# Adding the down projections' results to the residual by accumulating DMAs instead of VectorE

## The chip, the core and the metric

The kernel runs on one core of a Trainium2 chip. A core has a matrix engine (TensorE, PE in the profile, with its weight loads as PEld), a vector engine (VectorE, DVE), a scalar engine (ScalarE, ACT), GpSimd (POOL), and a queue processor (SyncE, SP). Each engine works through its own instruction list in order and waits on semaphores of the others. Data moves between the chip's memory and the on-chip SBUF, and inside SBUF, by 16 DMA engines; a transfer can be issued from SP, ACT or POOL. TensorE writes its sums into eight PSUM banks of 128 partitions x 512 fp32.

The metric is the device time of one execution, in microseconds (us), lower is better. Three runs of the kernel before took 1739.26, 1739.81 and 1739.86 us; the median is 1739.81 us. A separate execution was profiled.

## The reference

One layer on an input of 256 tokens x 2048 columns, fp32: a half-step SwiGLU feed-forward block, a mixer, a second half-step feed-forward block, and a final norm. The change touches only the line that adds a feed-forward block's result to the residual `x`, which runs twice:

```python
def swiglu_ffn(x, w_gate, w_up, w_down):
    return (jax.nn.silu(x @ w_gate) * (x @ w_up)) @ w_down

x = x + 0.5 * swiglu_ffn(rms_norm(x, ffn1_norm), ffn1_w_gate, ffn1_w_up, ffn1_w_down)
...                                    # mixer: x = x + y @ w_out
x = x + 0.5 * swiglu_ffn(rms_norm(x, ffn2_norm), ffn2_w_gate, ffn2_w_up, ffn2_w_down)
return rms_norm(x, final_norm)
```

`w_gate` and `w_up` are 2048 x 5632, `w_down` is 5632 x 2048.

## The kernel before

The residual stays on chip for the whole run, in one SBUF tile `xres` of 128 partitions x 2 token halves `t` x 2048 columns, cut into four column chunks `c` of 512. So one piece `xres[:, t, c]` is 128 x 512 fp32, 256 KB.

All weights are read once, as 1 MB blocks `raw` of 512 x 512, issued from SP. Each block is split for precision into a high part `hi` (a cast on ScalarE, two instructions of 128 x 1024) and a low part `lo` (a subtraction on VectorE, one instruction of 128 x 2048); TensorE multiplies with both (`multiply`). So ScalarE and VectorE must deliver a split block for every few microseconds of TensorE's work, and `raw` and split tiles come from pools of two to five buffers.

A feed-forward block `ffn(tag, ...)` runs through the 5632 hidden columns in six parts: a first chunk of 512, then five stages `s` of 1024. Each stage computes gate and up products with a seven-multiplication scheme (`seven`). After the stages `s` = 0, 2, 4 `down(last)` multiplies the hidden columns gathered so far with their rows of `w_down`, and adds half of the result to the residual. There are thus six down stages, three for each block. One down stage does, in the order of the code:

1. `product` for column chunk `c` = 0: two banks `ps_d`, one for each token half; then `update(0, t, ps)`.
2. `seven_of` prepares the sums of hidden blocks for the seven-multiplication scheme (`hspare` and eight `hs` tiles).
3. `seven` for the chunks 1 and 2 at once, in four banks `a`, `c`, `e`, `d`. On the way ScalarE copies four intermediate sums out of the banks (`snap`: `s1`, `s5`, `u2`, `u3`). When two banks of a chunk are complete (`done`, here `add`), `update` adds the bank and its snapshots to the residual: chunk 1 takes bank `c` with `u2` and bank `e` with `u3` and `s5`, chunk 2 takes bank `d` with `s1` and bank `a` alone.
4. `product` for `c` = 3 and `update(3, t, ps)`.

So in each down stage VectorE runs 12 instructions `xres = 0.5 * part + xres`: eight with a bank and four with a snapshot as the part.

`hspare`, `hs`, the snapshots and several tiles of the gate and up products are allocated with `keep(...)`, from one pool of 13 tiles of 128 x 512 fp32. A new tile waits until one of the 13 has had its last reader.

Instructions are not issued strictly in the order of the code: a planner orders each engine's list by program priority and by planned durations, and it places the semaphore waits. Only where `Engine.pinned` is true does an instruction keep its place in program order: in the opening, and from the last `product` of the second block on.

In the last down stage of each block `update` also calls `after(c, t)`. In the first block that is `to_mixer`, which defers the mixer norm's work on this chunk: squares of `xres` on ScalarE (`junk_nm`), and TensorE transposes of `xres` (`pt_nm`), which the mixer's first products read. In the second block it is `last`: squares on ScalarE (`junk_f`), for chunks 0 to 2 a VectorE scaling of `xres` by the final gain `fin`, after chunk 2 a partial sum `pre` and its root on ScalarE, and for chunk 3 the rest of the final norm and the stores of the output.

Of the kernel before, what the change touches and what calls it, by code (L numbers as in the profile page):

```python
# [12 lines left out]
AF = mybir.ActivationFunctionType  # L13
ALU = mybir.AluOpType
# [9 lines left out]
CW = 512  # L24
NC_D = D // CW
# [23 lines left out]
def hybrid_block(ctx: ExitStack, tc: tile.TileContext, a: dict, out: bass.AP):  # L49
    nc = tc.nc  # L50
    Engine.pinned = False
    dve, act, pe = (Engine(tc, e) for e in (nc.vector, nc.scalar, nc.tensor))
# [29 lines left out]
    def bank(name):  # L82
        return psum.tile([P, 512], F32, tag="ps", name=name)
# [74 lines left out]
    def load(src, name, pieces=((0, UK),), loaded=None, kept=False):  # L158
        if kept is None and extra and not turn_of["hold"]:
            turn_of["raw"] += 1  # L160
            kept = turn_of["raw"] % 5 > 2
        if kept:
            raw = extra[1].tile([P, UK, CW], F32, tag="kept", name=f"raw_{name}", bufs=2)
        else:
            raw = raws.tile([P, UK, CW], F32, tag="raw", name=f"raw_{name}")
        for i, e in pieces:
            nc.sync.dma_start(raw[:, i:e, :], src[i * P : e * P].rearrange("(j p) c -> p j c", p=P))
            if loaded:
                loaded(i)
        return raw  # L170

    def parts_of(raw, name, pieces=((0, 2), (2, UK)), split=None):
        pool, bufs = splits, 2
        if extra:
            turn_of["split"] += 1
            if turn_of["split"] % 3 == 0:
                pool, bufs = extra[0], 1
        hi = pool.tile([P, UK, CW], F32R, tag="hi", name=f"hi_{name}", bufs=bufs)
        lo = pool.tile([P, UK, CW], F32R, tag="lo", name=f"lo_{name}", bufs=bufs)
        for i, e in pieces:  # L180
            if split:
                split(i)
            act.copy(hi[:, i:e, :], raw[:, i:e, :])
            if split:
                dve.tensor_tensor(lo[:, i:e, :], raw[:, i:e, :], f32(hi[:, i:e, :]), op=ALU.subtract)
        if not split:
            dve.tensor_tensor(lo, raw, f32(hi), op=ALU.subtract)
        return [(hi[:, j, :], lo[:, j, :]) for j in range(UK)]
# [8 lines left out]
    def multiply(targets, blk, apart=False, middle=None):  # L197


        more = dict(skip_group_check=True) if apart else {}  # L200
        for ps, st, begin, _ in targets:
            for j in range(UK):
                pe.matmul(ps, st[j][0], blk[j][0], start=begin and j == 0, stop=False, **more)
                pe.matmul(ps, st[j][1], blk[j][0], start=False, stop=False, **more)
        if middle:
            middle()
        for ps, st, _, end in targets:
            for j in range(UK):
                pe.matmul(ps, st[j][0], blk[j][1], start=False, stop=end and j == UK - 1, **more)
# [141 lines left out]
    def quad(tile):  # L351
        return tile.rearrange("p (j c) -> p j c", j=UK)

    def seven(w, rows, cols, sf, xs, name, keep, done, between=None, ready=None):


        a, c, e, d = (bank(f"ps_{name}_{n}") for n in "aced")

        def get(u, n, kept=False):
            src = w[u * UK * P : (u + 1) * UK * P, cols[n] : cols[n] + CW]  # L360
            return load(src, f"{name}_{u}{n}", kept=kept)

        (r0, r1), two = rows, len(xs) > 1
        w11, first = ready or (get(r0, 0, True), None)
        w12 = get(r0, 1, True)
        b2, w22 = get(xs[0][0], 1), get(r1, 1)
        b3 = get(xs[1][0], 1) if two else None
        a2, w21 = get(xs[0][0], 0), get(r1, 0)
        a3 = get(xs[1][0], 0) if two else None

        def snap(ps, n):
            s = keep(f"{n}_{name}")
            act.copy(s, ps)
            return s

        def product_of(i, raw, ps, begin=False, end=True, blk=None):
            multiply([(ps, sf[i], begin, end)], blk or parts_of(raw, f"{name}_p{i}"), True)

        def usual(i, raw, n, *targets):

            blk = parts_of(raw, f"{name}_x{i}{n}")
            multiply([(ps, stationary(xs[i][1], t), b, z) for ps, t, b, z in targets], blk, True)

        product_of(0, w11, a, True, blk=first)
        s1 = snap(a, "s1")
        dve.tensor_tensor(w11, w12, w11, op=ALU.subtract)
        product_of(4, w11, c, True)
        s5 = snap(c, "s5")
        if between:
            between(0)  # L390
        usual(0, b2, 1, (e, 1, True, not two), (c, 0, False, False))
        if between:
            between(1)
        dve.tensor_tensor(w11, w22, w11, op=ALU.subtract)
        product_of(5, w11, a)
        u2 = snap(a, "u2")
        if between:
            between(2)
        if two:
            usual(1, b3, 1, (e, 1, False, True), (c, 0, False, False))  # L400
        dve.tensor_tensor(w12, w22, w12, op=ALU.subtract)
        product_of(6, w12, a)
        u3 = snap(a, "u3")
        done(1, 1, e, [u3, s5])
        product_of(2, w22, c)
        done(0, 1, c, [u2])
        usual(0, a2, 0, (d, 0, True, False), (a, 1, False, False))
        dve.tensor_tensor(w11, w21, w11, op=ALU.subtract)
        product_of(3, w11, a, end=not two)
        if two:  # L410
            usual(1, a3, 0, (a, 1, False, True), (d, 0, False, False))
        done(1, 0, a, [])
        product_of(1, w21, d)
        done(0, 0, d, [s1])

    def ffn(tag, norm, after, opening=False):
        with (
# [5 lines left out]
            wg, wu, wd = (a[f"ffn{tag}_w_{s}"][0] for s in ("gate", "up", "down"))  # L423

            def keep(name, dt=F32):
                return fp.tile([P, CW], dt, tag="keep", name=name, bufs=13)

            hidden = {}
# [24 lines left out]
            units, vs, sf, ready = [], {}, {}, []  # L453
# [36 lines left out]
            ps = {(m, t): bank(f"ps_{m}{tag}_0_{t}") for m in "gu" for t in range(NT)}  # L490
# [161 lines left out]
            xs = list(enumerate(units))[2:]  # L652
            turn_of["hold"] = False

            def down(last):
                us = sorted(set(hidden) | {w[0] for w in waiting})
                m, n = us[-2:]

                def update(c, t, *parts):
                    xr = xres[:, t, c * CW : (c + 1) * CW]  # L660
                    for p in parts:
                        dve.scalar_tensor_tensor(xr, p, 0.5, xr, op0=ALU.mult, op1=ALU.add)
                    if last:
                        after(c, t)

                for c in (0, 3):
                    end = last and tag == 2 and c == NC_D - 1
                    ps = product(
                        wd, c, us[:-2] + [n, m], hidden.get, f"d{tag}_{m}_{c}", end,
                        (lambda i: settle()) if c == 0 else None,  # L670
                    )
                    Engine.pinned = end
                    for t in range(NT):
                        update(c, t, ps[t])
                    if c == 0:
                        sh = {}
                        seven_of(
                            sh, hidden[m], hidden[n],
                            {(t, i): turned[u, t] for t in range(NT) for i, u in ((0, m), (1, n))},
                            quad(keep(f"hspare{tag}_{m}")),  # L680
                            [[quad(keep(f"hs{tag}_{m}_{i}_{z}", F32R)) for z in range(2)] for i in range(4)],
                        )()
                        got = {}

                        def add(t, b, ps, tiles):
                            got[t, b] = [ps] + tiles
                            if (0, b) in got and (1, b) in got:
                                for i in range(NT):
                                    update(2 - b, i, *got[i, b])

                        if tag == 1 and m == 5:
                            prepare()
                        seven(wd, (m, n), (2 * CW, CW), sh, [(u, hidden[u]) for u in us[:-2]], f"d{tag}_{m}", keep, add)
                hidden.clear()
                turned.clear()

# [78 lines left out]
    with tc.tile_pool(name="mixer", bufs=1) as mp, tc.tile_pool(name="mixw", bufs=2) as mw:  # L775
# [180 lines left out]
        for i, (use, part, half) in enumerate(order):  # L956
            ps = columns(w_in, part * (D // 2) + half * CW, nm.xT, f"in_{part}_{half}")
# [15 lines left out]
        for c in range(NC_D):  # L973
            cs = slice(c * CW, (c + 1) * CW)
            for g in range(2):
                if c == 0 and g == 1:
                    flush()
                ps = product(w_out, c, (2 * g, 2 * g + 1), yT.__getitem__, f"o{c}_{g}")
# [9 lines left out]
                for t in range(NT):  # L988
                    xr = xres[:, t, cs]
# [81 lines left out]
```

## Time and profile before

| | |
|---|---|
| median of 3 runs | 1739.81 us (1739.26 to 1739.86) |
| the profiled execution | 1741.48 us |
| its span, from the first to the last instruction | 1739.7 us |
| mean granted TensorE clock | 0.999 |
| last down stage of the first block | about 625 to 712 us |
| last down stage of the second block | about 1645 to 1731 us |

The profile is a record of one execution. Busy time counts an engine's instructions, without the issuing of DMAs from SP and ACT. A row of instructions reads: line, engine, operation, output<-inputs, shape, count, then busy us in all, mean ns of one, and the idle time of the engine just before them with what ended it. Nearly all instructions carry line 42, the line of the helper that records them, so they are told apart by their tiles; `ps_d` are the banks of the products for chunks 0 and 3, `ps_d_a`, `ps_d_c`, `ps_d_e`, `ps_d_d` those of the seven-multiplication scheme in a down stage.

### The profile page before, as it was taken

How to read it: one execution, taken by the hardware profiler on the slowest of the kernel's cores; microseconds unless marked ns; L12 is line 12 of the kernel's file. 1: busy time of each engine (PE TensorE's matmuls, PEld its weight loads, DVE VectorE, ACT ScalarE, POOL GpSimd, SP SyncE). 2: the span in 40 equal slices, each digit the busy share in tenths (PEclk: the TensorE clock that was granted, in tenths of full speed). 3: DMA queues.
4: the chain of work that ended last, by engine and by line, in shares of the span. 5: the costliest groups of instructions: out<-in, count | busy, mean ns of one | idle time of the engine just before them, and what ended most of it. 6: DMA issues, size and time to landing. Idle time of an engine off the chain costs nothing. (4 is left out here: it accounts for less than half of the span.)

```text
span 1739.7 us, 20328 instructions
## 1 busy us (share of the span) xinstructions
PE 1721.9 (99%) x8035; PEld 1436.1 (83%) x8035; DVE 1485.2 (85%) x1233; ACT 1042.1 (60%) x1345; POOL 6.9 (0%) x32
## 2 busy tenths in 40 slices
PE   8999999999999999999999999999999999999997
PEld 6888888888888888888888888888788888888886
DVE  7998999889789898687986668989799888899895
ACT  6765566656466656565655555656556664656654
POOL 1000000000000000000000000000000000000000
PEclk9999999999999999999999999999999999999999
DMA  8564665575466656555556663575475546555742
GB/s 299 191 213 145 218 214 197 182 254 205 159 209 203 199 188 216 172 170 194 177 189 209 224 203 129 199 243 185 160 252 201 206 144 231 193 194 194 255 174 104
DMA packets 173920, 343.24 MB, mean 197 GB/s; under 512 B 5636, under 2 KB 8064, under 8 KB 173696
## 3 DMA queue, kind: packets, MB, share of 16 engines
q1 hardware_dynamic: 173360, 340.82, 57.2%
q8 instruction: 63, 1.03, 0.2%
q10 hardware_dynamic: 144, 1.05, 0.1%
q14 instruction: 33, 0.27, 0.0%
q0 software_dynamic: 320, 0.07, 0.0%
HBM read 339.82 MB, written 2.10 MB: 197 GB/s over the span
## 5 line engine op out<-in xcount | busy, mean ns | idle before, releaser
L42 ACT CAST hi_g_p<-raw_g 128x1024 fp32r<-128x1024 f32 x132 | 134.3, 1049 | 97.8 <-DVE raw_g L42 27.6
L42 ACT CAST hi_u_p<-raw_u 128x1024 fp32r<-128x1024 f32 x140 | 140.8, 1047 | 73.1 <-DVE raw_u L42 26.8
L42 DVE TENSOR_TENSOR lo_g_p<-raw_g,hi_g_p 128x2048 fp32r<-128x2048 f32 x66 | 150.2, 2285 | 30.2 <-ACT hi_g_p L42 29.9
L42 DVE TENSOR_TENSOR lo_u_p<-raw_u,hi_u_p 128x2048 fp32r<-128x2048 f32 x70 | 159.0, 2286 | 19.3 <-ACT hi_u_p L42 18.9
L42 PE MATMUL ps_d<-hi_d,h 128*128 128x512 f32 x704 | 168.0, 390 | 0.0
L42 PEld LDWEIGHTS ps_d<-hi_d,h 128*128 128x128 f32 x704 | 131.5, 188 | 27.0
L42 PE MATMUL ps_in<-xT_nm,hi_in 128*128 128x512 f32 x640 | 153.3, 391 | 0.0
L42 PEld LDWEIGHTS ps_in<-xT_nm,hi_in 128*128 128x128 f32 x640 | 117.4, 188 | 23.3 <-ACT tha L42 0.3
L42 ACT CAST hi_d<-raw_d 128x1024 fp32r<-128x1024 f32 x88 | 88.2, 1047 | 68.2 <-PE ps_u_d L42 22.4
L42 DVE TENSOR_TENSOR lo_d<-raw_d,hi_d 128x2048 fp32r<-128x2048 f32 x44 | 100.6, 2290 | 31.0 <-ACT hi_d L42 31.0
L42 DVE TENSOR_TENSOR lo_in<-raw_in,hi_in 128x2048 fp32r<-128x2048 f32 x40 | 91.3, 2286 | 38.8 <-ACT hi_in L42 38.2
L42 ACT CAST hi_in<-raw_in 128x1024 fp32r<-128x1024 f32 x80 | 80.0, 1045 | 67.1 <-PE ps_in L42 45.8
L42 ACT CAST hi_d_p<-raw_d 128x1024 fp32r<-128x1024 f32 x84 | 84.3, 1047 | 50.2 <-DVE raw_d L42 39.4
L42 ACT CAST hi_g_x<-raw_g 128x1024 fp32r<-128x1024 f32 x80 | 81.3, 1048 | 47.5 <-PE ps_g_c L42 25.3
L42 DVE TENSOR_TENSOR lo_d_p<-raw_d,hi_d_p 128x2048 fp32r<-128x2048 f32 x42 | 95.4, 2286 | 11.8 <-ACT hi_d_p L42 11.7
L42 ACT CAST hi_u_x<-raw_u 128x1024 fp32r<-128x1024 f32 x80 | 80.5, 1047 | 33.9 <-PE ps_u_c L42 21.8
L42 DVE TENSOR_TENSOR raw_u<-raw_u,raw_u 128x2048 f32<-128x2048 f32 x40 | 91.6, 2290 | 9.0 <-DMA raw_u<-in_ffn_w_up_dram 8.3
L42 DVE TENSOR_TENSOR lo_g_x<-raw_g,hi_g_x 128x2048 fp32r<-128x2048 f32 x40 | 91.3, 2284 | 5.5 <-ACT hi_g_x L42 5.3
L42 DVE TENSOR_TENSOR raw_g<-raw_g,raw_g 128x2048 f32<-128x2048 f32 x37 | 84.5, 2286 | 9.3 <-DMA raw_g<-in_ffn_w_gate_dram 8.9
L42 DVE TENSOR_TENSOR lo_u_x<-raw_u,hi_u_x 128x2048 fp32r<-128x2048 f32 x40 | 91.4, 2284 | 0.8 <-ACT hi_u_x L42 0.5
L42 PE MATMUL ps_d<-lo_d,h 128*128 128x512 f32 x352 | 87.3, 389 | 0.0
L42 PEld LDWEIGHTS ps_in<-xT_nm,lo_in 128*128 128x128 f32 x640 | 82.1, 191 | 3.1
(391 smaller groups left out, 3592.2 us busy)
## 6 DMA issues: line engine op xcount, KB each, us to landing
raw_d<-in_ffn_w_down_dram SPq DMA_DIRECT2D x88, 1024.0 KB, 5.1
raw_u<-in_ffn_w_up_dram SPq DMA_DIRECT2D x87, 1024.0 KB, 5.2
raw_g<-in_ffn_w_gate_dram SPq DMA_DIRECT2D x86, 1024.0 KB, 5.2
raw_in<-in_w_in_dram SPq DMA_DIRECT2D x40, 1024.0 KB, 5.0
raw_o<-in_w_out_dram SPq DMA_DIRECT2D x16, 1024.0 KB, 5.1
xres<-in_x_dram SPq DMA_DIRECT2D x4, 512.0 KB, 7.6
raw_u<-in_ffn_w_up_dram SPq DMA_DIRECT2D x2, 512.0 KB, 9.3
raw_g_first<-in_ffn_w_gate_dram SPq DMA_DIRECT2D x1, 1024.0 KB, 11.9
```

The lines of the kernel that those rows point to most:

```text
L42: ins = getattr(self.engine, name)(*args, **kwargs)
```

## The change

For all pieces but `c` = 3 of the last down stage of either block (`last` is true for stage `s` = 4 of both), `update` no longer uses VectorE. ScalarE writes half of the bank into a new tile `half` of the 13-tile pool, and GpSimd issues one DMA for each part (first the snapshots, then `half`), which adds the part to the piece of `xres`. The snapshots of a down stage are halved as ScalarE takes them out of the banks (`scale=0.5`), so they can be added as they are. `after(c, t)` is called as before, right behind, and reads what the DMAs left.

```diff
-    def seven(w, rows, cols, sf, xs, name, keep, done, between=None, ready=None):
+    def seven(w, rows, cols, sf, xs, name, keep, done, between=None, ready=None, scale=None):
...
         def snap(ps, n):
             s = keep(f"{n}_{name}")
-            act.copy(s, ps)
+            if scale:
+                act.activation(s, ps, AF.Copy, scale=scale)
+            else:
+                act.copy(s, ps)
             return s
...
-                def update(c, t, *parts):
+                def update(c, t, ps, *tiles):
                     xr = xres[:, t, c * CW : (c + 1) * CW]
-                    for p in parts:
-                        dve.scalar_tensor_tensor(xr, p, 0.5, xr, op0=ALU.mult, op1=ALU.add)
+                    if last and c == NC_D - 1:
+                        dve.scalar_tensor_tensor(xr, ps, 0.5, xr, op0=ALU.mult, op1=ALU.add)
+                    else:
+                        half = keep(f"half{tag}_{m}_{c}_{t}")
+                        act.activation(half, ps, AF.Copy, scale=0.5)
+                        for p in (*tiles, half):
+                            nc.gpsimd.dma_start(xr, p, accum_op=ALU.add)
                     if last:
                         after(c, t)
...
-                        seven(wd, (m, n), (2 * CW, CW), sh, [(u, hidden[u]) for u in us[:-2]], f"d{tag}_{m}", keep, add)
+                        seven(wd, (m, n), (2 * CW, CW), sh, [(u, hidden[u]) for u in us[:-2]], f"d{tag}_{m}", keep, add, scale=0.5)
```

## The prediction, made before the changed kernel ran

> **What bounds the kernel now.** First the page's busy times, then the engines' busy time by stretches (the first 10 us, the body, the end), then TensorE's and its weight loads' waits inside the body.
>
> ```profile
> PE 1721.9 (99%) x8035; PEld 1436.1 (83%) x8035; DVE 1485.2 (85%) x1233; ACT 1042.1 (60%) x1345; POOL 6.9 (0%) x32
> ...
> 10.00:1725.00 1715.00, 1711.80 (x7997) 1428.07 (x7997) 1476.99 (x1212) 1033.11 (x1327) 1.05 (x16) 1.00 0.58 197
> 1725.00:1739.70 14.70, 5.85 (x26) 4.50 (x24) 5.15 (x14) 4.28 (x10) 0.00 (x0) 0.83 0.39 143
> ...
> PE ps_d_a L42 <- DVE lo_d_p L42: 1.1, 2, 0.9
> PE ps_g_c L42 <- DVE lo_g_p L42: 0.7, 1, 0.7
> PE ps_g_a L42 <- ACT hi_g_p L42: 0.3, 1, 0.3
> ...
> PEld ps_d_a L42 <- DVE lo_d_p L42: 2.6, 4, 1.3
> PEld ps_d_a L42 <- ACT hi_d_p L42: 0.7, 4, 0.2
> ```
>
> TensorE is busy for 1711.80 of the body's 1715.00 us, at a granted clock of 1.00. So 3.2 us are idle there, and that is the most that any relief of VectorE can return in the body (0.18% of the span). The row that the change can help directly is `ps_d_a <- lo_d_p`: TensorE waits for VectorE's splits in the down stages, 1.1 us by its own row, 2.6 us by the weight loads' row. The weight loads run ahead of the matmuls, so only the smaller is surely lost time. The end stretch holds the last chunk's norm and stores; chunk 3 of the last stage stays as it is, so it changes only if something earlier arrives late.
>
> VectorE at 85% looks like a second bound, but TensorE's three rows sum to 2.1 us, and one of them is ScalarE's: nearly all of VectorE's lateness is hidden.
>
> **What is removed.** The residual's additions on VectorE:
>
> ```profile
> L42 DVE SCALAR_TENSOR_TENSOR xres<-ps_d,xres x24: 677/682/692, 159.8 to 1730.9; 128x512 f32<-128x512 f32 x24
> ...
> L42 DVE SCALAR_TENSOR_TENSOR xres<-u_d,xres x12: 680/684/687, 179.6 to 1694.8; 128x512 f32<-128x512 f32 x12
> L42 DVE SCALAR_TENSOR_TENSOR xres<-s_d,xres x12: 677/682/692, 180.8 to 1713.7; 128x512 f32<-128x512 f32 x12
> ...
> L42 DVE SCALAR_TENSOR_TENSOR xres<-ps_d_e,xres x6: 680/684/692, 168.8 to 1688.0; 128x512 f32<-128x512 f32 x6
> ...
> L42 DVE SCALAR_TENSOR_TENSOR xres<-ps_d_a,xres x6: 678/686/692, 190.8 to 1705.8; 128x512 f32<-128x512 f32 x6
> ```
>
> With the banks `c` and `d` (six each, like `e` and `a`) that is 24 + 12 + 12 + 4 x 6 = 72; four stay (chunk 3 of the two last stages). 68 x 0.683 = 46 us leave VectorE. Two of them stand just ahead of the stretch where TensorE waits for `lo_d_p`, so I take the gain between 0 and 2.6 us, and as value 1.3, near the 1.1 us of TensorE's own row: half of the waits' chain is the splits themselves, which stay.
>
> **What ScalarE gets.** 48 - 4 = 44 new copies with a scale from a bank, and a scale on 24 snapshots. The nearest rows are the snapshot itself and an activation from a bank:
>
> ```profile
> L42 ACT COPY u_d<-ps_d_a x12: 574/579/589, 173.6 to 1690.1; 128x512 f32<-128x512 f32 x12
> ...
> L42 ACT ACTIVATE z<-ps_g_a 128x512 f32<-128x512 f32 x10 | 6.0, 600 | 33.7 <-PE ps_g_a L42 33.7
> ...
> 1393.00:1480.00 87.00, 87.00 (x389) 72.12 (x388) 73.34 (x51) 47.22 (x54) 0.00 (x0) 1.00 0.53 183
> ```
>
> 44 x 0.58 to 0.60 = 26 us, some 4.7 us for each down stage of eight copies. The last row is the third down stage of the three in the second block's middle: of 87 us ScalarE is busy for 47, so there is room for it, and the 20 ns by which the two rows differ come to 0.5 us over 24 snapshots, all behind TensorE's sums. What is not free is the place: a copy becomes ready just when a bank ends, where ScalarE also casts the next block, and TensorE's weight loads waited 0.7 us for `hi_d_p` in four places already. One copy of 0.58 us ahead of one such cast in one stage gives 0.6; in all six 3.5; hidden everywhere 0. I take 0.6, since the waits of that row are 0.2 us or less each, so some slack is left.
>
> **What GpSimd and the DMA engines get.** 68 DMAs of 256 KB, each adding into its piece. Additions to one piece must follow one another, so a second waits for the first to land. No accumulating DMA is in this trace. The nearest rows are GpSimd's issues at the start, its landing times for 4 to 8 KB, and the output's 256 KB stores from SP:
>
> ```profile
> L108 POOL DMA_DIRECT2D rows_conv<-in_lru_conv_w_dram x1 | 0.5, 524 | 0.7 <-DMA rows_many<-in_mix_norm_dram 0.7
> ...
> DMA to landing us min/median/max: 4.9/5.4/6.0
> ...
> out_dram<-xres SPq DMA_DIRECT2D x4, 256.0 KB, 2.7
> ```
>
> So one addition takes 0.5 us of issue and then between 2.7 us (the size's row from another queue) and 6 us plus the size, some 8 us. I take 5.4, the median from the queue that is used. [...]
>
> Bandwidth: a down stage adds 12 x 0.26 = 3.1 MB, or 9.4 MB if reading the piece and writing it back count each, to the 15.9 MB that 87 us at 183 GB/s move. A DMA share of 0.53 becomes 0.63 to 0.84. It stays under 1, so I cost the weight loads at nothing.
>
> ```profile
> raw_d<-in_ffn_w_down_dram SPq DMA_DIRECT2D x88, 1024.0 KB, 5.1
> ...
> SPq L167 <- DVE lo_d L42: 138.1, 38, 7.6
> ```
>
> What hides them is that a block lands in 5.1 us and SP has been waiting for a free buffer, not for a transfer. If that cover were gone a load behind one addition would be late by 256 KB at 183 GB/s, 1.4 us.
>
> Buffers: right behind the second snapshot of `seven` the pool holds eight `hs`, `s1`, `s5` and the two `half` of chunk 0, that is 12 of 13; later `hs` tiles come free two by two with each product. A landing of 5.4 us fits, no wait.
>
> **Who reads a landed piece, and when.** In four of the six stages nobody does until the next down stage. In the two last stages ScalarE's squares do, and ScalarE works in order. From the first block's last stage (the first row) and the second's, in order of time; the last row is from the chain of waits, TensorE's last product, which starts where bank `d` ends:
>
> ```profile
> 648.38 0.63 ACT L42 ACTIVATE junk_nm<-xres 128x512 f32<-128x512 f32 x1 [1.02 <-DVE xres L42]
> ...
> 1668.64 0.63 ACT L42 ACTIVATE junk_f<-xres 128x512 f32<-128x512 f32 x1
> 1669.17 0.19 ACT L42 ACTIVATION_READ_ACCUMULATOR junk_f<-xres 128x1 f32 x1
> ...
> 1673.14 0.59 ACT L42 COPY s_d<-ps_d_c 128x512 f32<-128x512 f32 x1 [2.13 <-PE ps_d_c L42]
> ...
> 1674.75 1.98 PE L42 MATMUL ps_d_c<-hi_d_x,h 128*128 128x512 f32 x8
> ...
> 1690.09 0.59 ACT L42 COPY u_d<-ps_d_a 128x512 f32<-128x512 f32 x1 [2.54 <-PE ps_d_a L42]
> ...
> 1712.76 2.00 ACT L42 CAST hi_d<-raw_d 128x1024 fp32r<-128x1024 f32 x2 [2.25 <-PE ps_d L42]
> ...
> 1718.44 0.45 ACT L42 ACTIVATE root<-pre 128x1 f32<-128x1 f32 x2 [1.01 <-DVE pre L42]
> 1726.23 0.63 ACT L42 ACTIVATE junk_f<-xres 128x512 f32<-128x512 f32 x1 [7.34 <-DVE xres L42]
> ...
> 1709.09 21.77 PE ps_d L42 x96
> ```
>
> Chunk 0: the squares run at 1668.64. With the change ScalarE makes the two halves there instead, 2 x 0.58 us, until 1669.8, and the piece lands at 1669.8 + 0.5 + 5.4 = 1675.7. Behind the squares stands the copy of `s5` at 1673.14, which must end before TensorE goes on in bank `c` at 1674.75. If the planner leaves the squares ahead of that copy, it ends at 1675.7 + two squares of 0.63 + 0.19 + the copy's 0.6 = 1677.9, and TensorE loses 3.1 us; if it puts them behind, nothing. I take a third, 1.0 us, because the planner orders by planned durations and will see some of the landing time. The first block has the same pattern at 648.38, so 2 x 1.0 = 2.0 us.
>
> Chunk 1: the longest chain is three additions (`u3`, `s5`, `half`) to one piece from the end of `u3`'s copy at 1690.7, at 5.9 us each: 1708.4. That is ahead of the last cast at 1712.76, up to a landing of 6.8 us. Cost 0. Chunk 2: its last bank ends at 1709.09, half and one addition end at 1716, before the root at 1718.44, and that one has slack until 1726.23. Cost 0. The first block's transposes of these chunks come later still.
>
> **The sum**: -1.3 (splits earlier) + 0.6 (copies ahead of casts) + 2.0 (squares of chunk 0 waiting) = +1.3 us on the profiled execution's 1741.48 us (span 1739.7 and 1.8 around it). That execution lies 1.7 us above the median, so on the median: 1739.81 + 1.3 = 1741.1 us. About 0.2% (3.5 us) is what a measurement of this kernel can tell from no change.
>
> **The rivals.**
>
> *ScalarE's queue is held by landings* (slower). Place: the squares of chunk 0 in the two last stages, ahead of the copy of `s5`. [...] It decides from a landing of about 2.3 us on, if the squares stay ahead. [...] Against it: the planner may move the squares. [...]
>
> *Landings so late that the end waits for them.* It decides from 10 us on. At 12 us, chunk 0 costs 9.7 us twice, and the chain of chunk 1 ends at 1690.7 + 3 x 12.5 = 1728.2, so that the root and the last squares start some 4 us late; 19.4 + 4 + 0.6 - 1.3 = +22.7, 1762.5 us. For it only that no row shows what adding in a DMA costs; against it the 2.7 us row.
>
> *Only the relief counts*: the squares move, the copies hide, and the whole 2.6 us of the weight loads' row come back: 1737.2 us. Against it: the 1.1 us row, and that the same VectorE chain still carries the splits. If not even this shows, the time is 1739.8 us and VectorE's busy time alone falls.
>
> **How the numbers follow.** Forecast as summed 0.50 (its own range 1738 to 1745), ScalarE held 0.28, late end 0.07, relief alone 0.15. Predicted time 1741.1. The range runs from 1736.8 (all of the 3.2 us idle, less a little) to 1755, above the held queue's price, with half of the late end outside. Slower by over 0.2%: 0.28 + 0.07 and 0.08 of the forecast's upper part, 0.43. Faster by over 0.2%: at most 0.04, since 3.2 us is under the bound. Within: 0.53.
>
> **What would show it.** VectorE's busy time near 1439 us and ScalarE's near 1068; TensorE's wait for `lo_d_p` under 1 us. A landing time from GpSimd's queue of 3 to 8 us for 256 KB. Right behind the halves of chunk 0, ScalarE idle before `junk_nm` and `junk_f`, released by a DMA, and TensorE waiting for `s_d` in `ps_d_c` for 0 to 3 us. I am wrong if TensorE's idle time in the body stays at 3 us and the time still moves, if the weight loads land much later than their 5 us, if ScalarE waits for buffers of the 13-tile pool, or if additions take over 10 us.

## The result and the profile after

The changed kernel takes 1780.97 us (median of four runs, 1779.45 to 1781.18), beside 1739.84 us for the kernel before on the same chip: a ratio of 1.0235, 95% interval 1.0218 to 1.0253, 41 us slower. The prediction was 1741.1 us with a range up to 1755. One of the four runs of the kernel with tiles of zeros, below, took 9982 us and is left out of its time and its ratio.

First the page's rows of the profile after that answer to those shown of before: busy times, the new queue's row (packets, MB, share of 16 engines' span) and the issues (count, KB each, median us to landing).

```profile
PE 1737.3 (98%) x8035; PEld 1445.0 (81%) x8035; DVE 1447.2 (81%) x1165; ACT 1062.1 (60%) x1389; POOL 65.9 (4%) x100
...
q0 software_dynamic: 10112, 17.90, 5.7%
...
xres<-half POOLq DMA_DIRECT2D x44, 256.0 KB, 4.0
xres<-s_d POOLq DMA_DIRECT2D x12, 256.0 KB, 6.9
xres<-u_d POOLq DMA_DIRECT2D x12, 256.0 KB, 6.7
```

VectorE's and ScalarE's busy times moved the way that the prediction had them, and by somewhat less (to 1447 and 1062 us, predicted 1439 and 1068). TensorE's rose by 15 us with the same 8035 matmuls, which nothing in the change explains by itself. The body by stretches and TensorE's longest waits in it (in all, times, longest) say where the rest is:

```profile
10.00:1764.60 1754.60, 1726.93 (x7997) 1436.88 (x7996) 1438.77 (x1144) 1052.94 (x1371) 60.04 (x84) 0.99 0.63 203
```

```profile
PE ps_d L42 <- ACT hi_d L42: 8.8, 2, 5.9
PE ps_g_c L42 <- ACT s_g L42: 6.7, 2, 3.3
PE ps_d_a L42 <- ACT s_d L42: 4.8, 2, 2.4
PE ps_d_c L42 <- ACT hs L42: 2.1, 1, 2.1
PE ps_d_e L42 <- DVE lo_d_x L42: 1.9, 3, 1.1
```

The body grew by 39.6 us: 24.5 us of it TensorE is idle (27.7 after, 3.2 before), and 15.1 us it is busy longer with the same 7997 matmuls. The waits are few and long, and they stand in three places. The table shows, for each part of the kernel whose length changed, by how many us the time from its first product to the first product of the next part differs from before; its starts are those of before, and the last three columns belong to experiments below. The row of a last down stage runs from its four-bank part on and takes in chunk 3; in the second block it ends at TensorE's last product.

| part | start | after | order alone | vector in last | both |
|---|---|---|---|---|---|
| four-bank part of a down stage | 158.6 | +3.9 | -1.1 | +2.3 | -1.1 |
| gate stage | 206.1 | -0.5 | +5.6 | -0.5 | +1.8 |
| gate stage | 458.4 | +6.3 | +5.7 | +5.9 | +4.5 |
| last down stage, first block | 646.9 | +9.9 | +9.0 | 0.0 | 0.0 |
| four-bank part | 1179.2 | +3.7 | -0.5 | +2.5 | -0.5 |
| gate stage | 1226.0 | +6.3 | +4.5 | +6.4 | +4.9 |
| four-bank part | 1416.4 | +1.0 | 0.0 | +1.0 | 0.0 |
| last down stage, second block | 1667.5 | +9.8 | +7.3 | -0.6 | +0.7 |
| an up stage | 1119.6 | -0.5 | -0.4 | -0.6 | -0.6 |

**Place 1, the four-bank parts.** In order of time, two rows of before and then the same place after:

```profile
150.80 0.69 DVE L42 TENSOR_TENSOR hspare<-z,u_g 128x512 f32<-128x512 f32 x1
...
164.29 0.59 ACT L42 COPY s_d<-ps_d_c 128x512 f32<-128x512 f32 x1 [0.85 <-PE ps_d_c L42]
```

```profile
159.35 0.60 ACT L42 ACTIVATE half<-ps_d 128x512 f32<-128x512 f32 x1
160.10 0.68 DVE L42 TENSOR_TENSOR hspare<-z,u_g 128x512 f32<-128x512 f32 x1
...
169.57 0.58 ACT L42 ACTIVATE s_d<-ps_d_c 128x512 f32<-128x512 f32 x1
169.72 0.49 PE L42 MATMUL ps_d_a<-hi_d_p,hs 128*128 128x512 f32 x1 [2.38 <-ACT s_d L42]
...
170.20 3.34 PE L42 MATMUL ps_d_c<-hi_d_x,h 128*128 128x512 f32 x8
```

`hspare` and the `hs` tiles behind it were made while TensorE was still on chunk 0's product; now `hspare` comes 9.3 us later, right behind the second `half`. The whole preparation of `seven_of` falls into the time when TensorE wants it, the snapshots on ScalarE slip from 164.29 to 169.57, and TensorE waits. Its next eight matmuls then take 3.34 us instead of 1.98 (the prediction's row of before at 1674.75): the granted clock is 0.50 there from 170.75 us on.

**Place 2, chunk 1 of the last stages.** The first block's, in order of time, GpSimd's issues between ScalarE's and TensorE's instructions:

```profile
680.41 0.89 POOL L670 DMA_DIRECT2D xres<-u_d  x1 [4.59 <-ACT u_d L42]
...
688.73 0.86 POOL L670 DMA_DIRECT2D xres<-s_d  x1 [4.77 <-DMA xres<-u_d]
...
694.73 0.86 POOL L670 DMA_DIRECT2D xres<-half  x1 [5.15 <-issue]
...
702.63 0.63 ACT L42 ACTIVATE junk_nm<-xres 128x512 f32<-128x512 f32 x1 [10.53 <-DMA xres<-half]
...
704.34 6.57 PE L42 MATMUL ps_d<-hi_d,h 128*128 128x512 f32 x16 [5.92 <-ACT hi_d L42]
```

The piece that takes `u3`, `s5` and `half` is added to three times, at 680.4, 688.7 and 694.7, and is complete at 702.6: 8.3, 6.0 and 7.9 us an addition. ScalarE waits 10.5 us for it at the squares, with the casts of chunk 3's weights queued behind, so TensorE waits 5.9 us for `hi_d`, and then runs 16 matmuls in 6.57 us that took 3.8 before.

**Place 3, the seam into the next gate stage.** Windows of before and of after around the seam at 458 us (the columns: length, busy PE, PEld, DVE, ACT, POOL, granted clock, DMA share, GB/s), and how long the 1 MB gate blocks issued and landed between 425 and 480 us took:

```profile
440.00:450.00 10.00, 10.00 (x46) 8.26 (x45) 4.81 (x3) 3.99 (x4) 0.00 (x0) 1.00 0.70 245
450.00:460.00 10.00, 10.00 (x46) 8.29 (x45) 9.90 (x7) 4.00 (x4) 0.00 (x0) 1.00 0.01 2
...
DMA to landing us min/median/max: 5.0/5.1/5.4
```

```profile
440.00:450.00 10.00, 10.00 (x45) 8.27 (x45) 6.79 (x3) 5.77 (x8) 1.76 (x2) 1.00 1.02 274
450.00:460.00 10.00, 10.00 (x46) 8.27 (x45) 3.08 (x2) 2.00 (x2) 0.00 (x0) 1.00 0.65 228
468.00:478.00 10.00, 6.67 (x18) 4.99 (x17) 7.14 (x4) 6.61 (x8) 0.00 (x0) 0.66 0.63 157
...
454.85 2.00 ACT L42 CAST hi_g_p<-raw_g 128x1024 fp32r<-128x1024 f32 x2 [9.09 <-DMA raw_g<-in_ffn_w_gate_dram]
...
472.43 3.78 PE L42 MATMUL ps_g_c<-hi_g_x,x 128*128 128x512 f32 x8 [3.33 <-ACT s_g L42]
...
DMA to landing us min/median/max: 5.0/8.5/9.9
```

Before, the blocks for the next stage are all there at 450 us and the DMA engines rest (share 0.01) until TensorE has used some. After, the seam is at 461.6 us, since place 1 has held it up by 3.2 us. Additions of chunks 1 and 2 fall into the 20 us from 430 to 450, where the share goes from 0.87 and 0.70 to 1.06 and 1.02 (the share sums the packets' times, so it can pass 1). The blocks take 8.5 us instead of 5.1 and are still arriving until 457.4. ScalarE waits 9.1 us for a block ahead of its first gate cast, which comes at 454.85 instead of 445.88; it works behind from there on, and its snapshot `s_g` holds TensorE 17.6 us later, again followed by half clock (0.66 in that window).

### The profile page after: what moved, and what is told of

Same layout as the page of the kernel before. It is cut to its first block, busy times and chain, and to the rows that moved or that the text cites. A ratio compares the mean times of both kernels' runs of the same rounds, so it can differ in the third digit from the quotient of the medians.

```text
span 1779.3 us, 20570 instructions
## 1 busy us (share of the span) xinstructions
PE 1737.3 (98%) x8035; PEld 1445.0 (81%) x8035; DVE 1447.2 (81%) x1165; ACT 1062.1 (60%) x1389; POOL 65.9 (4%) x100
## 5 line engine op out<-in xcount | busy, mean ns | idle before, releaser
L42 PE MATMUL ps_d<-hi_d,h 128*128 128x512 f32 x704 | 172.5, 398 | 8.8 <-ACT hi_d L42 8.8
L42 DVE TENSOR_TENSOR lo_g_p<-raw_g,hi_g_p 128x2048 fp32r<-128x2048 f32 x66 | 150.3, 2286 | 37.8 <-ACT hi_g_p L42 31.9
L670 POOL DMA_DIRECT2D xres<-half x44 | 38.3, 934 | 1386.2 <-ACT half L42 1341.7
```

Of the source, the lines that this page charges most:

```text
L42: ins = getattr(self.engine, name)(*args, **kwargs)
L670: nc.gpsimd.dma_start(xr, p, accum_op=ALU.add)
```

## The experiments

Three theories, one for each place. A: tiles are taken in program order, so `hspare` and `hs` stand behind the halves of chunk 0. B: in the last stages the landings hold ScalarE's queue. C: the additions take so much of the DMA engines' time that weight blocks come late. In all runs the kernel before ran beside them (1739.9 to 1740.5 us).

**Order alone.** Chunk 0's `update` is called behind `seven_of`:

```diff
-                    for t in range(NT):
-                        update(c, t, ps[t])
+                    if c == 3:
+                        for t in range(NT):
+                            update(c, t, ps[t])
                     if c == 0:
                         sh = {}
...
+                        for t in range(NT):
+                            update(c, t, ps[t])
```

> The change, with the two halves of chunk 0 written in the program behind the preparation of hspare and hs instead of ahead of it; nothing else. Theory A (order of buffers: hspare stands behind the halves in the 13-tile pool and so starts only after the first product): the seven-multiplication parts of the down stages 1, 3, 4, 5, 6 lose 3.9 + 1.0 + 3.7 + 1.1 + 4.9 = 14.6 us less, 1766 us; if the late weight loads behind the stages 2 and 4 (6.2 + 6.3) come from the same late start, 1754. Theory B (landings hold ScalarE's queue in the two last stages) alone: no change, 1781. Theory C (the DMA engines' added load alone makes weight loads late): no change, 1781.

Measured: 1771.41 us, ratio 1.0177 (1.0162 to 1.0192). `hspare` is back at its old place,

```profile
150.84 0.69 DVE L42 TENSOR_TENSOR hspare<-z,u_g 128x512 f32<-128x512 f32 x1
...
161.71 1.08 ACT L42 ACTIVATE half<-ps_d 128x512 f32<-128x512 f32 x2
```

and all three four-bank parts are on time or early (table, column "order alone"). But the gate stage at 206 us, on time in the changed kernel, is now late by 5.6: with the stall gone TensorE is at that seam 4.9 us sooner, and the last gate block lands only 2.4 us sooner. So the stalls cover each other. The four-bank parts give back 10.2 us, the last stages 3.4 and the two other seams 2.4, and the seam at 206 us takes 6.1 of it (3.4 of these are half clock behind a wait there).

**VectorE in the last stages.** All pieces of the two last stages go to VectorE again:

```diff
-                    if last and c == NC_D - 1:
+                    if last:
                         dve.scalar_tensor_tensor(xr, ps, 0.5, xr, op0=ALU.mult, op1=ALU.add)
+                        for p in tiles:
+                            dve.tensor_tensor(xr, xr, p, op=ALU.add)
```

> The change, but in both last stages all additions are VectorE's; the four other stages keep their 48 DMAs. Theory B: the waits of the squares on landings go, with TensorE's 5.9 and 2.9 us and the slow clock behind them (2.8 and 1.9), 1781 - 13.5 = 1767. Theory A: buffers order stays as it is in four stages and in the two last ones no half is taken, so 1.0 + 4.9 less, 1775. Both: 1761. Theory C: 48 of 68 DMAs stay, the two late gate stages (12.5) stay.

Measured: 1759.01 us, ratio 1.0113 (1.0096 to 1.0129). Both last stages are on time (0.0 and -0.6). The gate stages stay as after the change; the four-bank parts lose 2.3 and 2.5 us instead of 3.9 and 3.7, since the same stall is not followed by half clock in this run. The last stages were worth 20 us. This run also takes their halves away, so it does not tell A from B inside them.

**No DMA.** Each DMA of the changed kernel becomes an addition on VectorE; ScalarE's halves and their tiles stay:

```diff
-                            nc.gpsimd.dma_start(xr, p, accum_op=ALU.add)
+                            dve.tensor_tensor(xr, xr, p, op=ALU.add)
```

> The change with each DMA replaced by an addition on VectorE (ScalarE still halves into the 13-tile pool in the same program order). Theory A: the late start of hspare stays, 14.6 us of it, so at least 1754. Theory B and C: nothing waits for a landing and no load is added, so 1740 to 1742.

Measured: 1759.23 us, ratio 1.0109 (1.0094 to 1.0124). All six four-bank parts are late (5.2, 1.3, 2.2, 3.8, 2.2, 3.8) and no gate stage is. TensorE's longest group of waits is `ps_d_c <- ACT hs`, 9.1 us in six places. The six lose 18.5 us, more than in the changed kernel, as VectorE has its additions back as well. So A needs no DMA, and C does.

**Both remedies**, the order and VectorE in the last stages:

> e1 and e2 together: hspare first, and VectorE for both last stages; 48 DMAs stay. Theories A and B together: 1781 - 14.6 - 13.5 = 1753 if the two late gate stages have a cause of their own (C), about 1740 if they follow from the late start. A alone 1766, B alone 1767.

Measured: 1751.15 us, ratio 1.0063 (1.0048 to 1.0078). What is left (table, column "both") is the three gate stages, 11.2 us, and the gain that the change was to bring: -1.1 and -0.5 ahead of `ps_d_a`, -0.6 in an up stage.

**Tiles of zeros** on the kernel before: C by itself.

```diff
+            zeros = work.tile([P, CW], F32, tag="junkv", name=f"zeros_{tag}", bufs=1)
+            nc.gpsimd.memset(zeros, 0.0)
...
                     for p in parts:
                         dve.scalar_tensor_tensor(xr, p, 0.5, xr, op0=ALU.mult, op1=ALU.add)
+                    if not last:
+                        for p in parts:
+                            nc.gpsimd.dma_start(xr, zeros, accum_op=ALU.add)
```

> VectorE does all its additions as in the kernel before, and in the four down stages that are not last GpSimd adds a tile of zeros to the piece by an accumulating DMA once for each of them: 48 transfers of 256 KB, no new tile of the 13-tile pool in use, nothing on ScalarE, nobody reads the piece before the next down stage. The theory of the DMA engines (the additions take so much of their time that weight blocks come late at the seam into the next gate stage): the three gate stages behind a down stage that is not last start late, 2 to 6 us each as in the run with both remedies (1.8, 4.5, 4.9), in all 1747 to 1757 us. If what is left there comes from ScalarE's halves or from the pool, not from the transfers: 1739 to 1742 us.

Measured: 1755.90 us (median of three runs), ratio 1.0085 (1.0070 to 1.0100). The three gate stages are late by 4.7, 5.1 and 4.7, nothing else by more than 0.2. This kernel has neither halves nor a full pool; 48 transfers that nobody waits for cost 15 us, some 5 of them as half clock behind the waits (three stretches of 3.41 us).

**Plain copies** in the run with both remedies:

```diff
-                            nc.gpsimd.dma_start(xr, p, accum_op=ALU.add)
+                            nc.gpsimd.dma_start(xr, p)
```

> The run with both remedies, with plain copies in place of the accumulating transfers (the addition is left out there, the bytes and the number of transfers are the same). If the adding itself loads the DMA engines: landings of the pieces shorter than 4 us, the stretch of the first queue's time that they take about halved, the three late gate stages (1.8, 4.5, 4.9 us) shrink to below half, 1740 to 1746 us. If it is bytes and number of transfers alone that delay the weights: as with both remedies, 1751 us.

Measured: 1739.08 us, ratio 0.9993 (0.9984 to 1.0002); the gate stages -0.0, +0.7, 0.0. The queue's row of the run with both remedies, of zeros, and of plain copies:

```profile
q0 software_dynamic: 7232, 12.66, 4.1%
```

```profile
q0 software_dynamic: 7232, 12.66, 4.3%
```

```profile
q0 software_dynamic: 4160, 12.66, 1.9%
```

The same bytes take half the time, and the seams are on time to 0.7 us although the DMA share ahead of one still reaches 1.01 (from 420 to 430 us), so a full share alone did not make the weights late here. An addition is cut into 144 packets a transfer and a copy into 80 ((7232 - 320) / 48 and (4160 - 320) / 48, with the 320 packets of before), and costs 4.1% x 1749 / 48 = 1.5 us of all 16 engines, a copy 1.9% x 1738 / 48 = 0.7 us. The landings show less of it, and the forecast of less than 4 us did not come: the median for `half` is 4.0 us after the change, 6.4 with both remedies and 4.0 with plain copies.

**Folded**: order alone, with the snapshots added into `half` on VectorE and one DMA for each piece.

```diff
-                        for p in (*tiles, half):
-                            nc.gpsimd.dma_start(xr, p, accum_op=ALU.add)
+                        for p in tiles:
+                            dve.tensor_tensor(half, half, p, op=ALU.add)
+                        nc.gpsimd.dma_start(xr, half, accum_op=ALU.add)
```

> The run with hspare made ahead of chunk 0's halves, with the snapshots added into the half tile on VectorE, and one transfer per piece (44 in all instead of 68, no piece has more than one). The theory that landings hold ScalarE at chunk 1 of the last stages (three additions to a piece in a row, some 7 us each): the waits of the squares there fall from 5 to 10 us to below 2, and the two last stages, late by 9.0 and 7.3 us with the order alone, are late by less than 3 each. The theory of the DMA engines: the gate stages behind a down stage, late by 5.6, 5.7 and 4.5, shrink by about a third. In all about 1754 us. If it isn't the chains: the last stages stay late by 7 or more, 1765 us or above.

Measured: 1748.70 us, ratio 1.0046 (1.0032 to 1.0060). The last stages are late by 1.2 and 0.5 instead of 9.0 and 7.3, the gate stages by 1.2, 3.9 and 1.0 instead of 5.6, 5.7 and 4.5. The longest waits of the squares fell to 2.3 and 4.5 us:

```profile
ACT junk_f L42 <- DMA xres<-half: 8.4, 5, 4.5
ACT junk_nm L42 <- DMA xres<-half: 5.7, 3, 2.3
```

So B is for the most part the row of three additions to one piece; the run also has 24 transfers fewer, and its landings of `half` are shorter too (a median of 4.1 us, 4.5 with the order alone). One wait is above the forecast of 2 us, and yet the last stages lose 1.2 and 0.5 us. The gate stages at 206 and 1226 us shrank by far more than the third that was forecast, the one between them by about that, and the time is below the 1754 us.

**Chunk 0 alone** through ScalarE and DMAs, in the stages that are not last, behind `seven_of`:

```diff
-                    if last:
+                    if last or c:
```

> The run with both remedies, but of the stages that are not last only chunk 0 goes through ScalarE and DMAs (8 transfers), all else is VectorE's as in the kernel before. All three theories: nothing late at the seams, since chunk 0 lands some 25 us ahead of the seam and two transfers stand where twelve did, and VectorE's relief at the splits ahead of the seven-multiplication scheme stays (-1.1, -0.5): 1738 to 1740 us. If even two transfers, or the work on ScalarE at that place, delay something: 1741 us or more.

Measured: 1738.56 us (median of 11 runs) beside 1740.45, ratio 0.9992 (0.9983 to 1.0000). Eight transfers far from a seam harm nothing that shows, and the relief of VectorE stays. This is the lowest ratio of a kernel that still adds, 1.4 us, but its interval touches 1: no gain that is clear of the noise.

**Is it the engines' time or the adding?** Three runs with copies that fill the same engine time, and one with additions that take half of it. The first issues each copy twice:

```diff
-                            nc.gpsimd.dma_start(xr, p)
+                            for _ in range(2):
+                                nc.gpsimd.dma_start(xr, p)
```

> The run with plain copies, each copy issued twice (96 transfers of 256 KB; the addition is left out as there). If it is the DMA engines' time that counts, whatever fills it: 96 copies take about the time of 48 additions (q0 near 4% of 16 engines), the seam has about 17 us more to move per stage, and the three gate stages behind a down stage are late again, 2 to 5 us each, 1747 to 1756 us. If it is something of the adding itself (the reading of the piece, the traffic at SBUF beside VectorE and ScalarE) and not the time of the engines: no gate stage is late, 1738 to 1742 us.

Measured: 1740.19 us, ratio 1.0001 (0.9992 to 1.0011); q0 at 3.9%, gate stages -0.3, +1.0, +0.2. By the expectation this spoke for the adding itself. The trace gives another reading: two copies to one piece wait for each other (GpSimd waits for landed copies of `half` in 23 places, 51.6 us in all and 6.2 at the longest), and a part of them came behind the seam. Windows there of the single copies, then of the double ones:

```profile
450.00:460.00 10.00, 10.00 (x45) 8.28 (x45) 9.90 (x5) 4.87 (x6) 1.07 (x2) 1.00 0.08 30
460.00:470.00 10.00, 9.57 (x42) 7.59 (x41) 8.52 (x5) 6.86 (x8) 0.00 (x0) 1.00 0.44 146
```

```profile
450.00:460.00 10.00, 10.00 (x46) 8.29 (x45) 9.90 (x5) 4.87 (x6) 2.15 (x4) 1.00 0.29 112
460.00:470.00 10.00, 9.29 (x42) 7.35 (x41) 8.53 (x5) 6.86 (x8) 1.07 (x2) 1.00 0.63 193
```

The engines do the same in both but for GpSimd's issues, and the DMA share stands 0.2 higher from 450 to 470 us, when the weights are already there. The second makes each copy twice as wide instead:

```diff
-                            nc.gpsimd.dma_start(xr, p)
+                            nc.gpsimd.dma_start(xres[:, :, c * CW : (c + 1) * CW], p.unsqueeze(1).to_broadcast([P, 2, CW]))
```

> The run with plain copies, each copy made twice as wide: it writes its part to the piece of both token halves, 512 KB in one transfer, 48 transfers as before (the addition is left out). In the run with each copy issued twice the second copies came behind the seam, since two copies to one piece wait for each other; here all the bytes move at the same time as the additions did. If the DMA engines' time ahead of the seam is what counts, whatever fills it: q0 near 4%, the three gate stages behind a down stage late by 2 to 5 us each, 1746 to 1755 us. If the delay is the adding's own (the piece read and written back) and not time of the engines: no gate stage late by more than 1 us, 1738 to 1742 us.

Measured: 1741.30 us, ratio 1.0007 (0.9997 to 1.0016); q0 at 3.8%, gate stages -0.5, +1.3, +1.1. Here both token halves are written by each transfer, so five transfers stand in one row at chunk 1, and again a part of the traffic may come late. This run too came out against the forecast of the engines' time, so the third, which takes that row away, is its test:

```diff
-                            nc.gpsimd.dma_start(xr, p)
+                            pair = xres[:, t, c // 2 * 2 * CW : (c // 2 + 1) * 2 * CW].rearrange("p (a w) -> p a w", a=2)
+                            nc.gpsimd.dma_start(pair, p.unsqueeze(1).to_broadcast([P, 2, CW]))
```

> The wide copies again, but each writes its part to the pieces of two neighbouring chunks (0 and 1, or 2 and 3) of one token half, so that no transfer waits for more others than the additions did; in the run before, the longer rows of transfers to one piece had moved part of the traffic behind the seam (the addition is left out). If the DMA engines' time ahead of the seam counts, whatever fills it: the gate stages late by 2 to 5 us each, 1745 to 1753 us. If it is the adding's own: late by about 1 us each at most, 1739 to 1742 us.

Measured: 1757.09 us, ratio 1.0094 (1.0079 to 1.0109), above the forecast of 1745 to 1753; q0 at 3.8%, gate stages +5.2, +6.6, +5.9. At the seam at 206 us the two runs can be held side by side, since both gate stages start at 205.0 us and their blocks are issued at the same times. GpSimd's queue in the 20 us ahead of the seam, a window, and how long the gate blocks took to land, of the wide copies in a row, and then of those that do not wait for each other:

```profile
q0 software_dynamic: 417, 1.51, 19.9%
...
195.00:205.00 10.00, 10.00 (x46) 8.29 (x45) 9.71 (x5) 3.53 (x6) 2.18 (x3) 1.00 0.79 293
...
DMA to landing us min/median/max: 7.8/10.1/10.4
```

```profile
q0 software_dynamic: 718, 2.61, 34.2%
...
195.00:205.00 10.00, 10.00 (x46) 8.29 (x45) 4.58 (x2) 4.58 (x5) 1.45 (x3) 1.00 1.04 386
...
DMA to landing us min/median/max: 10.0/12.5/15.7
```

The two have the same bytes, packets and queue share over the whole kernel, and differ only in which pieces they write, and so in when the bytes move. In the first the splits go on (VectorE busy for 9.71 us from 195 to 205); in the second 1.1 MB more moves ahead of the seam, the blocks land later, VectorE is busy for 4.58 us, and the gate stage is 5.2 us late. The last run halves the additions of zeros:

```diff
-                            nc.gpsimd.dma_start(xr, zeros, accum_op=ALU.add)
+                            nc.gpsimd.dma_start(xr[:, : CW // 2], zeros[:, : CW // 2], accum_op=ALU.add)
```

> The run with tiles of zeros, but each addition covers only the left half of the piece (128 KB): as many transfers and as many in a row as before, each still read, added and written back, with half the bytes. If the DMA engines' time ahead of the seam counts: q0 near 2%, about what the plain copies took, and the gate stages late by less than 1 us each, 1739 to 1743 us. If adding as such delays the weights whatever its size: late by more than 3 us each, 1750 us or more.

Measured: 1746.73 us, ratio 1.0037 (1.0025 to 1.0050); q0 at 2.4%, gate stages +2.1, +0.6, +1.5 (and +0.7 in the up stage behind the second). Between the two forecasts: 4.2 us of the 14.5 of whole additions, for 2.4 in place of 4.3% of queue time. A part of the gap is the clock: whole additions had three stretches of half clock, half ones none. Plain copies with 1.9% cost 0.7.

The seam at 206 us in all these runs, which reach it at 204.9 to 205.1 us, with zeros at 206.3 and 206.4:

| run | GpSimd's queue, share of 16 engines in the 20 us ahead | gate stage late by | of it half clock |
|---|---|---|---|
| plain copies | 15.1% | 0.0 | 0 |
| copies twice | 19.9% | -0.3 | 0 |
| wide copies in a row | 19.9% | -0.5 | 0 |
| half additions of zeros | 20.7% | +2.1 | 0 |
| additions of zeros | 31.9% | +4.7 | 1.7 |
| wide copies not in a row | 34.2% | +5.2 | 1.7 |
| both remedies | 35.8% | +1.8 | 0 |

So C holds in these runs: transfers ahead of a seam made the weights late, whether they added (zeros, 14.5 us) or only copied (the last wide copies, 17.7 us). An addition took twice the engines' time of a copy of the same bytes (1.5 and 0.7 us), and plain copies of the change's own bytes cost 0.7 us. That the engines' time in the 20 us ahead is the measure fits the order of the runs at the seam at 206 us, but for the one with both remedies; it is thin there between 19.9 and 20.7%. At the seam at 458 us it is not shown: there the wide copies in a row have the larger share ahead of the seam (27.1%, late by 1.3), and those not in a row the smaller (22.8%, late by 6.6, 3.4 of it half clock). How much room there is at each seam stays open, and so does why both remedies lose less at 206 us than zeros do (1.8 and 4.7, of which 1.7 is half clock).

## Why the prediction was wrong, point by point

The time moved the way that was forecast, upwards, but not by the forecast's mechanism: its +2.0 us for the squares of chunk 0 did not come. Three steps that put a term at nothing failed, and half clock, which no step had, came on top.

- *Splits earlier, -1.3 (between 0 and 2.6).* Right. Where nothing else was late (both remedies, plain copies) two four-bank parts give -1.1 and -0.5, -1.6 us in all. The -0.6 of an up stage is not shown to belong to it: with tiles of zeros, where VectorE keeps its additions, that stage gives -0.4 too.
- *Halves ahead of ScalarE's casts, +0.6.* Not contradicted: the plain copies have all of ScalarE's work of the stages that are not last and lose 0.7 us at one seam, which can also be the copies' load on the DMA engines. Each half takes 0.59 us, as costed.
- *"A landing of 5.4 us fits, no wait" for the 13-tile pool.* Failed. The step counted how many tiles live at once (12 of 13), and not in which order they are asked for. `hspare` and `hs` are asked for behind the halves, and these can be made only when chunk 0's banks end. Price by the rows of the table 8.6 us (3.9, 3.7, 1.0) and 3.4 in the last stages (9.9 and 9.8 against 9.0 and 7.3); moving the call alone removes it. What holds `hspare` back, the pool or the planner's priority, both of which follow program order, was not told apart.
- *"It stays under 1, so I cost the weight loads at nothing."* Failed, with 12.6 us at two seams in the changed kernel and 15 us by itself. The step took a mean over 87 us of stage, 0.53 to 0.84; from 430 to 450 us, ahead of a seam, the share already stood at 0.87 and 0.70, and with the additions it passed 1. The fallback, 1.4 us for a load behind one addition, was the size of one addition, but several stand there, and ScalarE's first gate cast came 9.0 us later than before while the seam came 3.2 later.
- *Squares of chunk 0, 2 x 1.0 us.* Did not come: these additions landed in 3.3 to 3.4 us, the squares waited 0.55 us at most, and the snapshots come later anyway. In order of time, after the change:

```profile
658.31 0.86 POOL L670 DMA_DIRECT2D xres<-half  x1 [0.71 <-ACT half L42]
...
661.79 0.63 ACT L42 ACTIVATE junk_nm<-xres 128x512 f32<-128x512 f32 x1 [0.55 <-DMA xres<-half]
```

- *"Chunk 1 ... Cost 0", up to a landing of 6.8 us.* Failed, and is the largest term: 20 us in two stages. The chain of three additions was right, but it was held against the wrong reader. The step took ScalarE's last cast, at 1712.76; the squares of chunk 1 stand in ScalarE's list ahead of all casts of chunk 3, and TensorE wants the first of these at 1708.93. In order of time, before:

```profile
1697.27 0.63 ACT L42 ACTIVATE junk_f<-xres 128x512 f32<-128x512 f32 x1
...
1700.72 1.99 ACT L42 CAST hi_d<-raw_d 128x1024 fp32r<-128x1024 f32 x2
...
1708.93 3.79 PE L42 MATMUL ps_d<-hi_d,h 128*128 128x512 f32 x16
```

  And the same place after:

```profile
1745.12 0.63 ACT L42 ACTIVATE junk_f<-xres 128x512 f32<-128x512 f32 x1 [6.56 <-DMA xres<-half]
...
1746.83 5.52 PE L42 MATMUL ps_d<-hi_d,h 128*128 128x512 f32 x16 [2.91 <-ACT hi_d L42]
```

  TensorE's product starts 1.71 us behind the square's start in both last stages, so from the end of `u3`'s copy the chain had 16.7 us. The forecast's own three times 5.9 us would have been 1.0 us late; measured were 19.6 and 22.6, and TensorE waits 2.9 and 5.9 us. With the half clock behind these waits (1.7 and 3.4 us) that is 13.9 of the 20 us; the rest was not taken apart, but the order alone takes back 3.4 us. The rival of ScalarE held by landings named this mechanism, but set it at chunk 0. No run shows a source for the held queue's price that the range's upper end, 1755 us, stands above; what the runs show is ScalarE waiting 6.6 and 10.5 us for a piece of chunk 1.
- *What no step had.* Most stalls cost more than their wait, since the granted clock was 0.50 for 3.4 or 6.8 us behind them: 15.1 of the 39.6 us. The list of what would show the prediction wrong names late weight loads, and these came (8.5 us at the seam); it does not name the clock.

## What to carry to other kernels

A transfer is not free because the mean DMA share leaves room (with tiles of zeros it was 0.61 from 10 to 1764.6 us, and the kernel lost 15 us): look at the share in the 20 us ahead of the point where the next weights must be there, and multiply the number of new transfers in that stretch by their engine time, which for 256 KB was 1.5 us of all 16 engines for an addition and 0.7 for a copy. A share of 1 alone is not yet the sign: with plain copies it was 1.01 from 420 to 430 us, fell to 0.79 from 440 to 450, and the gate stage behind the seam was late by 0.7 us. When a result is given a tile from a shared pool, see what is asked for behind it in program order and was ready earlier. Where several additions go to one piece, fold them on a compute engine first, and count the whole row of landings (here three of 6.0 to 8.3 us) against the first reader on an in-order engine.

## What the runs showed of the hardware that was not expected

- **Half clock after short stalls.** In the changed kernel the body's matmuls took 15.1 us longer. Windows of the clock column, the first around the stall in place 1, the second right behind the one in place 2:

```profile
168.00:174.90 6.90, 5.18 (x15) 3.88 (x16) 5.94 (x5) 3.47 (x7) 0.85 (x1) 0.75 0.48 145
...
704.30:711.00 6.70, 6.66 (x18) 5.23 (x19) 5.47 (x3) 5.69 (x7) 1.75 (x2) 0.57 0.09 14
```

  A stall of 2.38 us is followed by half clock, with 0.75 over 6.9 us (the mean of half of the stretch at 0.5 and the rest at 1), one of 5.92 us by 0.57 over 6.7 us. The body has seven such stretches, each of 3.41 or 6.83 us, and their starts lie whole multiples of 3.41 us apart (the first three at 170.75, 471.12 and 703.23 us, 88 and 68 of them); before it has none. The length of the stall alone does not decide: with VectorE in the last stages the same stall of 2.38 us in the same place stays at full clock,

```profile
168.00:174.90 6.90, 5.22 (x22) 4.12 (x23) 6.47 (x6) 4.17 (x8) 0.85 (x1) 1.00 0.52 148
```

  and over all runs the shortest that half clock followed was 1.91 us (no DMA, 171.0 us) and the longest that it did not 3.55 us (both remedies, 1236.5 us). The clock is 0.50 in all seven stretches of the changed kernel and 1.00 in the rest of its body; what decides whether half clock follows a stall was not shown.
- **The price of adding in a DMA.** For 256 KB inside SBUF 1.5 us of all 16 engines, against 0.7 for a copy. In the changed kernel an addition moves in 128 packets of 2 KB, of 178 ns each at the median. Per packet of data, a copy's 64 of 4 KB come to some 170 ns (1.9% of 16 x 1738.4 us over 48 x 64 packets), and the 128 of 1 KB of an addition of half the bytes to some 110 ns (2.4% of 16 x 1743.5 us over 48 x 128), both estimates from the queue's share. Landings of `half` in the changed kernel lie between 3.3 and 10.5 us, and an issue on GpSimd takes 0.85 to 1.5 us, 0.86 at the median, not the 0.5 of the opening's rows. Plain copies were issued in 0.54 us beside nearly the same work of VectorE (busy for 1454.9 us from 10 to 1764.6 us, and for 1455.2 with both remedies, where an issue takes 0.86 us and more); what makes an addition's issue longer was not shown. The plain copies of `half` landed with a median of 4.0 us.
- **Stalls that cover each other.** Removing place 1's stall ahead of the seam at 206 us (3.9 us, and a gain of 1.1) made that gate stage late by 5.6 us, 3.4 of it half clock: TensorE came to the seam 4.9 us sooner and the last gate block landed 2.4 us sooner, so the first stall had been giving the weights time to arrive.
